# 352 tokens dense and 160 gathered in the expert layer, instead of 384 and 128, with part of the gathers among the gates

## The chip, the core and the metric

The kernel runs on one core of one Trainium2 chip. The metric is the device time of one execution in microseconds (us), read as the median of several runs. All input and output lies in the chip's memory; the span of a profile goes from the first to the last instruction.

## What is computed

Two transformer blocks on 512 tokens of width 1024, one after the other, in float32. The change touches only the last part, the expert layer. There each token chooses 128 of 16384 experts (8 heads, 16 choices each); an expert is a pair of numbers (i1, i2) from 0 to 127, with a gate g.

```
def peer_ffn(x, w_q, sub_keys, expert_u, expert_v):
    ...
    v1, i1 = lax.top_k(s1, P_TOPK)
    v2, i2 = lax.top_k(s2, P_TOPK)
    cand = (v1[..., :, None] + v2[..., None, :]).reshape(T, P_HEADS, P_TOPK * P_TOPK)
    vals, ci = lax.top_k(cand, P_TOPK)
    e = (take(i1, ci // P_TOPK) * N_KEYS + take(i2, ci % P_TOPK))
    g = jax.nn.softmax(vals, axis=-1)
    ...
        a = jnp.einsum('cd,ckd->ck', xc, expert_u[ec])
        w = (gc * jax.nn.gelu(a)).astype(x.dtype)
        return jnp.einsum('ck,ckd->cd', w, expert_v[ec])
```

The layer's output is added to the residual h.

## The kernel before

Up to about 1000 us the two blocks run (mixer, attention, projections). `peer` then works on the 512 tokens in two ways.

**Dense.** For the first NT = 384 tokens all 16384 experts are computed as 128 tiles of 128 experts. An up tile (`up_tile`) loads 512 KB of `pu`, splits it into a high and a low part (`whi` on ACT, `wlo` on DVE), runs 24 matmuls of 384 columns (lines 85 to 87, three products for each of 8 slices of the width) and applies gelu. A down step (loop over e) loads 512 KB of `pv`, splits it likewise, multiplies the tile's activations by a dense matrix of gates (`hm`, line 1544), splits the product (`xh`, `xl`, tiles `p`) and runs 18 matmuls of 512 columns into six banks `y0` to `y5`: three blocks of 128 tokens, two halves of the width, three products. 37 of the 128 up tiles are computed ahead and put away in memory (`ud`, read again as `gl`), 11 more (AHEAD) are kept on the chip (`gt`).

**The gates** (`gates`, L1443 to L1470) make the dense matrix of gates out of the choices. For each token a one-hot matrix of i1 times g and a one-hot matrix of i2 are built and multiplied on PE (L1466). One `hot` tile, a ring of six buffers named `r4`, holds four tokens: its half for i2 is built on DVE eight tokens at a time (`short`, L1457) and cast on ACT (L1460), its half for i1 by four `tensor_scalar` on DVE (L1463). ACT copies the product out of PSUM (L1467, `big`). Every 32 tokens the result (2 MB, `wd`) is written to memory; in the down loop four experts' rows of it are read again per four steps (`big<-wd`, L1537). The gates run between the last 30 of the 48 early up tiles; the other 18 lie in the loop over query projections before them.

**Gathered.** For the last 128 tokens only the chosen experts are fetched: an indirect DMA on POOL (L1493) brings one row of 4 KB for each of 128 tokens, 256 times: 128 times from `pun`, each followed by a multiply and reduce on DVE against the tokens (L1498), and 128 times from `pv`, each followed by a multiply-add on DVE into `idx` (L1508). The gathered rows use the same ring `r4` of six buffers. `work.advance` deals them out over the down loop, up to 86% over its first 80 steps, the rest over 36 more; all of them begin after the gates.

The order of instructions on each engine is fixed when the kernel is built, by a scheduler with its own table of durations; on the chip every engine takes its list in order. Weights come by SP's queue into `wraw` (3 and 2 buffers).

Of the kernel before, what the change touches and what calls it, by code (L numbers as in the profile page):

```python
# [44 lines left out]
class Builder:  # L45
# [574 lines left out]
    def attention2(self, wk, ps, h, hg):  # L620
# [480 lines left out]
        xd = self.dram.tile([128, 1024], F32, name="xd")  # L1101
# [17 lines left out]
        for b in range(4):  # L1119
# [12 lines left out]
            if b % 2 == 1:  # L1132
                for m in range(4):
# [4 lines left out]
                    for j in range(2):  # L1138
                        ts = slice(b * 128 - 128, b * 128 + 128)
                        k = 2 * m + j  # L1140
                        self.split_scaled(pt[:, j * 256:j * 256 + 256], self.gains[:, 3, k:k + 1], xn[0][k][:, ts], xn[1][k][:, ts])
        nc.gpsimd.tensor_tensor(n2b, n2b, xs[3], op=ALU.mult)
        nc.sync.dma_start(xd, n2b)
# [112 lines left out]
    def peer(self, hd, xn, xd):  # L1256
# [3 lines left out]
        NT = 384  # L1260
        AHEAD = 11
        AWAY = 37
        NREST = 4
        with ExitStack() as s5:
# [172 lines left out]
            def gates():  # L1437


                for b in range(NT // 128):  # L1440
# [3 lines left out]
                    bs = slice(b * 128, (b + 1) * 128)  # L1444
                    for n in (0, 2):
                        nc.scalar.copy(iT[n][:, bs], pt[:, n * 128:(n + 1) * 128])
                    second = wk.tile([128, 128, 8], BF16, tag="oh2", name="second", bufs=4)
                    nc.scalar.copy(second, pt[:, 128:256, None].to_broadcast([128, 128, 8]))
                    for tg in range(4):
                        wt = T("big", 2, shape=(128, 128, 32))  # L1450
                        for t4 in range(8):
                            hot = T("r4", 6, shape=(128, 2, 4, 128))
                            t0 = 128 * b + 32 * tg + 4 * t4
                            if t4 % 2 == 0:
                                short = wk.tile([128, 8, 128], BF16, tag="p", name="short", bufs=6)
                                of = second[:, t0 - 128 * b:t0 - 128 * b + 8]
                                nc.vector.tensor_tensor(short.rearrange("p t (a c) -> p t a c", c=8),  # L1457
                                                        numbers.rearrange("p (a c) -> p a c", c=8)[:, None].to_broadcast([128, 8, 16, 8]),
                                                        of[:, :, None].to_broadcast([128, 8, 16, 8]), op=ALU.is_equal)
                            nc.scalar.copy(hot[:, 1], short[:, t4 % 2 * 4:t4 % 2 * 4 + 4])  # L1460
# [15 lines left out]
            def gathered():  # L1476
                i1, i2, g = chosen(3)
# [190 lines left out]
```

## Time and profile before

| | us |
|---|---|
| median of 3 runs | 2263.39 (2263.33 to 2266.34) |
| profiled execution, its own time | 2264.04 |
| its span | 2262.3 |
| PE busy | 2207.7 (98%) |
| DVE busy | 1657.4 (73%) |
| ACT busy | 1014.1 (45%) |
| POOL busy | 724.7 (32%) |

Matmuls overlap in the records, so what one costs is read from the distance between starts, not from its duration. The DMA share is the mean busy share of the 16 DMA engines. A timeline's third column group names engine, line, operation, the tile written and the tiles read.

### The profile page before, as it was taken

The numbers are of one execution on the slowest core, as the hardware profiler recorded it, in microseconds if no ns is written. First come the engines' busy times: TensorE is split into PE (matmuls) and PEld (weight loads), VectorE is DVE, ScalarE is ACT, GpSimd is POOL, SyncE is SP. The second block draws the span as 40 slices with busy tenths as digits, with TensorE's granted clock in tenths as the row PEclk, the third lists the DMA queues.
The fourth block names the chain that finished last, engine by engine and source line by source line (L and its number), as shares of the span: only waits on it lengthen the run. The fifth ranks groups of instructions, "written<-read, shape, count | busy, mean of one in ns | idle before, by whom it ended". The sixth has DMA issues, their size and how long they took to land.

```text
span 2262.3 us, 32117 instructions
## 1 busy us (share of the span) xinstructions
PE 2207.7 (98%) x11327; PEld 1927.8 (85%) x11327; DVE 1657.4 (73%) x3611; ACT 1014.1 (45%) x1781; POOL 724.7 (32%) x731
## 2 busy tenths in 40 slices
PE   7999999999999889989999999999999999999999
PEld 5888888888878757879999998999999999998887
DVE  7875666543357688769889986888888888888654
ACT  4544444432244578853237764333333333333332
POOL 1221111000013756735640002544445444444000
PEclk9999999999999999989999999999999999999999
DMA  4222222243333212154445667999999999999874
GB/s 131 80 80 84 84 77 82 88 136 94 94 96 119 87 49 80 65 178 130 133 137 176 250 214 295 352 339 349 338 337 345 333 336 347 344 334 351 271 230 126
DMA packets 171443, 439.57 MB, mean 194 GB/s; under 512 B 15121, under 2 KB 74001, under 8 KB 169745
## 3 DMA queue, kind: packets, MB, share of 16 engines
q1 hardware_dynamic: 129088, 296.00, 40.3%
q0 software_dynamic: 36864, 134.23, 16.1%
q10 hardware_dynamic: 5328, 7.28, 0.9%
q8 instruction: 89, 1.46, 0.3%
q14 instruction: 74, 0.60, 0.1%
HBM read 395.05 MB, written 41.35 MB: 193 GB/s over the span
## 4 chain that ended last, share of the span: by engine, by line
PE 88%; DVE 6%; ACT 2%; issue 2%; DMA 1%; POOL 1%; SPq 0%; DVEq 0%; POOLq 0%; ACTq 0%
PE mm L87 13%; PE mm L86 13%; PE mm L85 13%; PE y L85 8%; PE y L86 8%; PE y L87 8%; PE y L1466 4%; PE g L87 3%; PE g L86 3%; PE g L85 3%; PE s L377 2%; PE pt L403 2%; PE o L407 1%; PE o L406 1%; PE wo L86 1%
## 5 line engine op out<-in xcount | busy, mean ns | idle before, releaser
L66 ACT CAST whi<-wraw 128x1024 fp32r<-128x1024 f32 (+2 forms) x413 | 430.4, 1043 | 977.3 <-PE mm L86 395.3
L72 DVE TENSOR_TENSOR wlo<-wraw,whi 128x1024 fp32r<-128x1024 f32 x368 | 456.8, 1241 | 255.6 <-ACT whi L66 255.3
L87 PE MATMUL mm<-uh,wlo 128*128 128x384 f32 (+1 forms) x1616 | 578.1, 358 | 3.7 <-DVE wlo L72 3.7
L85 PE MATMUL mm<-uh,whi 128*128 128x384 f32 (+1 forms) x1616 | 580.0, 359 | 0.3 <-DVE ul L154 0.3
L86 PE MATMUL mm<-ul,whi 128*128 128x384 f32 (+1 forms) x1616 | 578.7, 358 | 0.0
L85 PEld LDWEIGHTS mm<-uh,whi 128*128 128x128 f32 x1616 | 304.5, 188 | 26.3 <-DVE ul L154 0.7
L87 PEld LDWEIGHTS mm<-uh,wlo 128*128 128x128 f32 x1616 | 304.5, 188 | 25.7 <-DVE wlo L72 4.0
L86 PEld LDWEIGHTS mm<-ul,whi 128*128 128x128 f32 x1616 | 304.6, 188 | 25.2
L85 PE MATMUL y<-whi,p 128*128 128x512 f32 x768 | 300.7, 392 | 0.2 <-ACT p L66 0.2
L86 PE MATMUL y<-wlo,p 128*128 128x512 f32 x768 | 300.4, 392 | 0.0
L87 PE MATMUL y<-whi,p 128*128 128x512 f32 x768 | 291.4, 390 | 0.0
L1493 POOL DMA_INDIRECT r<-pun_in,row x128 | 167.1, 1305 | 362.7 <-DVE act L1498 175.0
L1493 POOL DMA_INDIRECT r<-pv_in,row x128 | 171.1, 1337 | 185.3 <-DVE idx L1508 163.4
L72 POOL TENSOR_TENSOR wlo<-wraw,whi 128x1024 fp32r<-128x1024 f32 (+3 forms) x45 | 100.9, 2247 | 304.9 <-ACT whi L66 304.8
L87 PEld LDWEIGHTS y<-whi,p 128*128 128x128 f32 x768 | 144.2, 188 | 32.1
L85 PEld LDWEIGHTS y<-whi,p 128*128 128x128 f32 x768 | 144.2, 188 | 29.0 <-ACT p L66 0.6
L86 PEld LDWEIGHTS y<-wlo,p 128*128 128x128 f32 x768 | 144.3, 188 | 27.4
L1498 DVE CUSTOM_DVE_ANT_0 r<-r,val 128x1024 f32<-128x1024 f32 x128 | 153.9, 1220 | 13.5 <-DMA r<-pun_in,row 13.5
L1508 DVE SCALAR_TENSOR_TENSOR idx<-r,act,idx 128x1024 f32<-128x1024 f32 x127 | 162.9, 1283 | 1.1
L72 DVE TENSOR_TENSOR p<-p 128x384 fp32r<-128x384 f32 x128 | 71.3, 557 | 93.5 <-PE y L86 90.5
L382 ACT ACTIVATE p<-p,st 128x128 f32<-128x128 f32 (+3 forms) x160 | 89.7, 562 | 72.6 <-DVE st L381 71.0
L1463 DVE TENSOR_SCALAR r<-iota,iT,iT 128x128 f32<-128x128 f32 x384 | 102.6, 360 | 15.7 <-PE y L1466 15.7
(603 smaller groups left out, 3584.9 us busy)
## 6 DMA issues: line engine op xcount, KB each, us to landing
wraw<-w_in SPq DMA_DIRECT2D x145, 512.0 KB, 3.6
wraw<-pu_in SPq DMA_DIRECT2D x128, 512.0 KB, 5.4
wraw<-pv_in SPq DMA_DIRECT2D x128, 512.0 KB, 5.5
wd<-big SPq DMA_DIRECT2D x12, 2048.0 KB, 7.2
big<-wd SPq DMA_DIRECT2D x31, 768.0 KB, 7.3
ud<-gs ACTq DMA_DIRECT2D x37, 192.0 KB, 2.2
gl<-ud SPq DMA_DIRECT2D x37, 192.0 KB, 2.8
hd<-h SPq DMA_DIRECT2D x24, 256.0 KB, 2.3
```

What stands on the lines that cost most here:

```text
L66: nc.scalar.copy(hi, src)
L72: i = eng.tensor_tensor(lo, src, hi, op=ALU.subtract)
L85: mm(out, w[0], x[0], start=start, stop=False)
L86: mm(out, w[0], x[1], start=False, stop=False)
L87: mm(out, w[1], x[0], start=False, stop=stop)
L377: nc.tensor.matmul(s[:, :n], q[:, b], k[:, :n], start=t == 0, stop=t == len(qk) - 1)
L382: nc.scalar.activation(pi, pi, AF.Exp, bias=st[:, 0:1], scale=-1.0, accum_out=st[:, 1:2])
L1463: nc.vector.tensor_scalar(hot[:, 0, t], iota, i1, g, op0=ALU.is_equal, op1=ALU.mult)
L1466: nc.tensor.matmul(wp[:, t * 128:(t + 1) * 128], hot[:, 0, t], hot[:, 1, t], start=True, stop=True)
L1493: nc.gpsimd.indirect_dma_start(t, None, src, bass.IndirectOffsetOnAxis(ap=rows[n][:, s:s + 1], axis=0))
L1498: nc.vector.tensor_tensor_reduce(t, t, xn3, 1.0, 0.0, ALU.mult, ALU.add, act[:, s:s + 1])
L1508: nc.vector.scalar_tensor_tensor(yg[0], t, act[:, s:s + 1], yg[0], op0=ALU.mult, op1=ALU.add)
```

## The change

`NT` becomes 352, and the last 32 of the third block's tokens join the gathered ones. Up tiles run matmuls of 352 columns, the third token block of a down step has 96 tokens, and the gates have 88 hot tiles instead of 96 and 11 matrices to write instead of 12.

The 32 tokens are laid out as four quarters on 128 rows (`quarters`: row 32q + t holds token t's choices 32q to 32q + 31), so that 32 gathers from `pun` and 32 from `pv` do them; twelve small DMAs of 32x32 and four of 32x1024 set this up. A matmul with `fold` adds the four quarters, and the sum is added to `h` and written out. Then follow the 128 tokens as before. There are 320 gathers in all; `picked.advance` deals 15% of them (48) out over the 30 up tiles among the gates, then up to 85% over the 80 first down steps, and the rest over 45 more.

In the gates the half of a hot tile for i1 is built by ACT from a second `short` (a copy with scale g) for tokens 0 to 7 of every 16, and by DVE as before for the others.

```diff
-        nc.sync.dma_start(xd, n2b)
+        nc.sync.dma_start(xd[:128], n2b)
+        nc.sync.dma_start(xd[128:], xs[2][96:128])
...
-        NT = 384
+        NT = 352
+        INGATES = 0.15
...
                             if t4 % 2 == 0:
...
+                                s2 = short(1, t0 - 128 * b)
+                                s1 = short(0, t0 - 128 * b) if t4 % 4 == 0 else None
+                            half = t4 % 2 * 4
+                            nc.scalar.copy(hot[:, 1], s2[:, half:half + 4])
                             for t in range(4):
                                 i1, g = (iT[n][:, t0 + t:t0 + t + 1] for n in (0, 2))
-                                nc.vector.tensor_scalar(hot[:, 0, t], iota, i1, g, op0=ALU.is_equal, op1=ALU.mult)
+                                if s1 is None:
+                                    nc.vector.tensor_scalar(hot[:, 0, t], iota, i1, g, op0=ALU.is_equal, op1=ALU.mult)
+                                else:
+                                    nc.scalar.activation(hot[:, 0, t], s1[:, half + t], AF.Copy, scale=g)
...
+            def quarters(tag, src, dt=F32):
+
+                t = T(tag, 1, dt, (128, 32))
+                for q in range(4):
+                    nc.sync.dma_start(t[32 * q:32 * q + 32], src[96:128, 32 * q:32 * q + 32])
+                return t
...
+            def gathered():
+                rows = [quarters(f"rq{n}", r, I32) for n, r in enumerate(rows_of(2))]
+                g = quarters("gq", chosen(2)[2])
...
+                yield from gather(rows, xg, T("actq", shape=(128, 32)), g, part)
...
+                    nc.tensor.matmul(p, fold, part[:, cs], start=True, stop=True)
+                    nc.vector.tensor_tensor(h[96:128, cs], h[96:128, cs], p[96:128], op=ALU.add)
+                nc.sync.dma_start(self.out[352:384], h[96:128])
+                rows = rows_of(3)
+                xg = T("val", shape=(128, 1024))
+                nc.sync.dma_start(xg, xd[:128])
+                yg[0] = T("idx", shape=(128, 1024))
+                yield from gather(rows, xg, T("act", shape=(128, 128)), chosen(3)[2], yg[0])
...
+            picked = Work(gathered(), 320)
             for n, e in enumerate(rest_tiles):
                 work.advance((n + 1) / len(rest_tiles))
                 up_tile(e, "dve")
+                picked.advance((n + 1) / len(rest_tiles) * INGATES)
...
-                work.advance((e + 1) / steps * 0.86 if e < steps else 0.86 + (e + 1 - steps) / 36 * 0.15)
+                picked.advance(INGATES + (0.85 - INGATES) * (e + 1) / steps if e < steps else 0.85 + (e + 1 - steps) / 45 * 0.16)
```

What the scheduler makes of it is seen at three places. The first is PE at the end of the gates. `y` with `r` is a hot tile, `mm` an up tile, `y` with `whi,p` the first down step. Before:

```order
L87 MATMUL mm<-uh,wlo_13639 128x384
L1466 MATMUL y_13676<-r_13670 128x128 x4
L1466 MATMUL y_13690<-r_13682 128x128 x4
L1466 MATMUL y_13702<-r_13696 128x128 x4
L85 MATMUL mm<-uh,whi 128x384
...
L86 MATMUL mm<-ul,whi_13782 128x384
L85 MATMUL y_13741<-whi,p 128x512
```

And with the change, at the same place:

```order
L85 MATMUL mm<-uh,whi_13907 128x352
L1480 MATMUL y_13271<-r_13263 128x128 x4
L86 MATMUL mm<-ul,whi_13907 128x352
L87 MATMUL mm<-uh,wlo_13908 128x352
L1480 MATMUL y_13283<-r_13277 128x128 x4
L1480 MATMUL y_13335<-r_13325 128x128 x4
...
L1480 MATMUL y_13821<-r_13815 128x128 x4
L85 MATMUL y_13866<-whi,p 128x512
```

Before, the hot tiles come three at a time between up tiles, and a whole up tile stands between the last of them and the first down step. With the change the up tiles end earlier: 21 hot tiles (y_13283 to y_13821) stand behind the last matmul of an up tile, with nothing between them, and the first down step follows at once.

The second place is DVE in the middle of the gates, with the change. `actq` is the multiply and reduce of a gathered row; before, these stand in the down loop and the gates hold only the other kinds.

```order
L1475 TENSOR_SCALAR r_11976<-iota,iT_11436,iT_11438 128x128 x4
L1457 TENSOR_TENSOR short<-numbers,eights 128x1024 x2
L1521 ISA r_11956,actq<-r_11956,val 128x1024
L1521 ISA actq 128x1
L1521 ISA r_11959,actq<-r_11959,val 128x1024
L1457 TENSOR_TENSOR short<-numbers,eights 128x1024
L72 TENSOR_TENSOR wlo_12802<-wraw,whi_12801 128x1024
```

In the whole stretch from the first `short` to the first down step's multiply, DVE has 176 `tensor_scalar` (380 before), 66 `short` (48), 24 `wlo` (22), 32 reduces and 14 multiply-adds of gathered rows (1 and 0).

The third place is DVE late in the down loop, at steps 95 and 96, before:

```order
L1544 TENSOR_TENSOR p<-gl,big 128x384
L72 TENSOR_TENSOR wlo<-wraw,whi 128x1024
L72 TENSOR_TENSOR p<-p 128x384
L1567 TENSOR_TENSOR r_21170<-r_21170,idx 128x512 x2
L1544 TENSOR_TENSOR p<-gl,big 128x384
```

And with the change, at steps 100 and 101:

```order
L1531 SCALAR_TENSOR_TENSOR idx<-r_20532,act,idx 128x1024
L1593 TENSOR_TENSOR p<-gl,big 128x352
L1531 SCALAR_TENSOR_TENSOR idx<-r_20567,act,idx 128x1024
L72 TENSOR_TENSOR wlo<-wraw,whi 128x1024
L72 TENSOR_TENSOR p<-p 128x352
L1531 SCALAR_TENSOR_TENSOR idx<-r_20602,act,idx 128x1024
L1531 SCALAR_TENSOR_TENSOR idx<-r_20637,act,idx 128x1024
```

Before, the last gathered row is consumed ahead of step 94's multiply, and 23 of the 256 stand behind step 80's. With the change the last one stands ahead of step 114's, and 54 of the 320 stand behind step 80's: 19 up to step 91's, 35 from there on.

## Rows read from the trace of the kernel before

**Rows 1.** Busy time by stage: us, then busy (count) per engine, PE clock, DMA share, GB/s

```profile
1000.00:1180.00 180.00, 179.94 (x991) 164.95 (x989) 153.44 (x809) 59.88 (x85) 98.04 (x103) 1.00 0.43 130
1214.00:1300.00 86.00, 86.00 (x655) 85.97 (x653) 86.00 (x264) 69.80 (x132) 0.00 (x0) 1.00 0.62 229
1500.00:1600.00 100.00, 100.00 (x509) 91.15 (x509) 82.45 (x121) 35.35 (x49) 47.91 (x37) 1.00 0.96 340
```

**Rows 2.** Who waited for whom, 1180 us to the end: total us, times, longest

```profile
DVE r L1498 <- DMA r<-pun_in,row: 13.5, 3, 7.9
...
PE mm L87 <- DVE wlo L72: 3.7, 1, 3.7
```

**Rows 3.** Timeline of PE: start us, duration us, engine, line, operation

```profile
1599.98 0.34 PE L87 MATMUL mm<-uh,wlo 128*128 128x384 f32 x1
...
1603.79 0.39 PE L85 MATMUL y<-whi,p 128*128 128x512 f32 x1
...
1607.91 0.33 PE L85 MATMUL mm<-uh,whi 128*128 128x384 f32 x1
...
1306.86 2.84 PE L1466 MATMUL y<-r 128*128 128x128 f32 x24
1309.45 0.42 PE L85 MATMUL mm<-uh,whi 128*128 128x384 f32 x1
...
765.46 0.28 PE L87 MATMUL f<-whi,cx 128*64 128x256 f32 x1
...
766.49 0.28 PE L87 MATMUL f<-whi,cx 128*64 128x256 f32 x1
```

**Rows 4.** Timeline of DVE among the gates

```profile
1233.17 6.25 DVE L1463 TENSOR_SCALAR r<-iota,iT,iT 128x128 f32<-128x128 f32 x24
1239.32 1.90 DVE L1457 TENSOR_TENSOR short<-numbers,second 128x1024 bf16<-128x1024 bf16 x3
1241.12 2.37 DVE L72 TENSOR_TENSOR wlo<-wraw,whi 128x1024 fp32r<-128x1024 f32 x2
```

**Rows 5.** Timeline of DVE and of its groups: a gathered row's reduce, and its multiply-add

```profile
1602.10 1.22 DVE L1498 CUSTOM_DVE_ANT_0 r<-r,val 128x1024 f32<-128x1024 f32 x1
...
L1508 DVE SCALAR_TENSOR_TENSOR idx<-r,act,idx 128x1024 f32<-128x1024 f32 x127 | 162.9, 1283 | 1.1
```

**Rows 6.** Timeline of ACT: among the gates, and scaled copies before them

```profile
1225.21 1.08 ACT L66 CAST whi<-wraw 128x1024 fp32r<-128x1024 f32 x1
1226.16 0.52 ACT L1382 ACTIVATE gs<-mm 128x384 f32<-128x384 f32 x1
...
1232.06 0.61 ACT L1467 COPY big<-y 128x512 f32<-128x512 f32 x1
1232.53 0.65 ACT L1460 CAST r<-short 128x512 f32<-128x512 bf16 x1
1233.05 0.61 ACT L1467 COPY big<-y 128x512 f32<-128x512 f32 x1
...
988.22 0.47 ACT L153 ACTIVATE uh<-s,gains 128x256 fp32r<-128x256 f32 x1
988.59 0.71 ACT L1131 ACTIVATE p<-h,r 128x512 f32<-128x512 f32 x1
```

**Rows 7.** DMA queues and gathers, 1500 to 2040 us: packets, MB, share; issues, us to landing

```profile
q0 software_dynamic: 27891, 101.55, 51.2%
q1 hardware_dynamic: 45172, 81.81, 44.2%
...
r<-pv_in,row POOLq DMA_INDIRECT x110, 6.6
r<-pun_in,row POOLq DMA_INDIRECT x85, 6.9
```

**Rows 8.** DMA queue of SP, 2140 to 2200 us: packets, MB, share of 16 engines

```profile
q1 hardware_dynamic: 9568, 13.10, 73.7%
```

**Rows 9.** Busy time of a stretch as in Rows 1, with the densest transfers

```profile
1400.00:1460.00 60.00, 56.32 (x276) 50.92 (x275) 47.32 (x71) 20.32 (x28) 26.99 (x19) 0.97 1.02 374
```

More of the change, by code (lines that the diff above doesn't have):

```diff
@@ L1437, in gates @@
             def gates():
-                for b in range(NT // 128):
+                for b in range(3):
                     pt = P("y2")
@@ L1443, in gates, with short @@
                         nc.tensor.transpose(pt[:, n * 128:(n + 1) * 128], t, self.ident)
-                    bs = slice(b * 128, (b + 1) * 128)
+                    nb = min(128, NT - b * 128)
                     for n in (0, 2):
[L1446 to L1449, printed above, removed]
+                        nc.scalar.copy(iT[n][:, b * 128:b * 128 + nb], pt[:, n * 128:n * 128 + nb])
+                    eights = [wk.tile([128, 128, 8], BF16, tag="oh2", name="eights", bufs=4) for _ in range(2)]
+                    for n in range(2):
+                        nc.scalar.copy(eights[n], pt[:, n * 128:n * 128 + 128, None].to_broadcast([128, 128, 8]))
+                    def short(n, t):
+                        x = wk.tile([128, 8, 128], BF16, tag="p", name="short", bufs=6)
+                        nc.vector.tensor_tensor(x.rearrange("p t (a c) -> p t a c", c=8),
+                                                numbers.rearrange("p (a c) -> p a c", c=8)[:, None].to_broadcast([128, 8, 16, 8]),
+                                                eights[n][:, t:t + 8, None].to_broadcast([128, 8, 16, 8]), op=ALU.is_equal)
+                        return x
+                    for tg in range(nb // 32):
                         wt = T("big", 2, shape=(128, 128, 32))
@@ L1474, in peer, with rows_of @@
             yg = [None]
[L1476 to L1477 removed]
+            def rows_of(b):
+                i1, i2, _ = chosen(b)
                 rows = []
[L1479 removed]
+                for n, (x, z) in enumerate(((i1, i2), (i2, i1))):
                     t = T("rf", 1, shape=(128, 128))
[L1481 removed]
+                    nc.vector.scalar_tensor_tensor(t, x, 128.0, z, op0=ALU.mult, op1=ALU.add)
                     ri = T(f"row{n}", 1, I32, (128, 128))
@@ L1521, in advance @@
                             self.done += c
-            work = Work(gates(), 3 * 32 * 0.8)
+            work = Work(gates(), NT // 4 * 0.8)
+            picked = Work(gathered(), 320)
             rest_tiles = list(first_tiles)
@@ L1531, in peer @@
             y = [[P(f"y{2 * b + c}") for c in range(2)] for b in range(3)]
-            work = Work(gathered(), 256 * 1.2)
             for e in range(128):
```

59 lines of the change are left out of this document (32 added, 27 removed).

## Prediction

> **What bounds the kernel now.** I read the busy times by stage first, then who waited for whom, then distances between starts. From 1000 us on PE is busy throughout: 179.94 of 180 us in the loop over queries, 86 of 86 among the gates, 100 of 100 in the down loop [rows 1]. Behind 1180 us it waited for DVE once, 3.7 us [rows 2], at the start of the down loop, where DVE itself waited for gathered rows, 13.5 us in three waits [rows 2]. So the expert layer's time is PE's own sum, and what shortens PE's list shortens the kernel, as long as no other engine comes out longer. Two are near: DVE, with 86 of 86 us in the first half of the gates and 82 of 100 later, and the DMA engines, with a share of 0.96 in the down loop against 0.62 among the gates [rows 1]. The change takes work from PE and gives work to ACT, DVE and DMA in just these stages.
>
> **What a matmul costs.** From 1599.98 to 1603.79 us lie 22 matmuls of 384 columns, 0.1732 us each, from there to 1607.91 us 18 of 512, 0.2289 each [rows 3]. No row has 352 columns. The line through 384 and 512 gives 0.1593, that through 256 (nine in 1.03 us, 0.1144 each [rows 3]) and 384 gives 0.1585. I take 0.159: 0.0142 less than now, 0.34 us for an up tile of 24. A record of a hot tile's matmul costs 0.108 (24 in 2.59 us [rows 3]), and a hot tile has eight of them, 0.86 us. The 18 matmuls of a down step keep their 512 columns: that one block has 96 tokens instead of 128 shortens only its weight load, so nothing is gained there.
>
> **Early up tiles.** 18 lie in the loop over queries, where PE is full and DVE has 27 us of 180 free [rows 1]: 18 x 0.34 = **-6.1**.
>
> **The gates.** Before, PE has 24 up tiles of 4.16 us and 96 hot tiles beside them: 99.8 + 82.9 = 182.7 us. DVE, counted from the order: 380 `tensor_scalar` at 0.256, 48 `short` at 0.60, 22 `wlo` at 1.19 [rows 4] and one gathered row make 153 us. ACT: 96 x 0.99 for the cast and the copy of a hot tile, some 23 `whi` at 0.95, as many gelus at 0.52 [rows 6] and three copies of 1024 elements make 132 us. PE is the longest by 30 us.
>
> With the change PE has 24 x 24 x 0.159 + 704 x 0.108 = 167.6 us. DVE: 176 x 0.256 + 66 x 0.60 + 24 x 1.19 + 32 reduces at 1.22 + 14 multiply-adds at 1.28 [rows 4, 5] = 170 us. ACT: 88 x 0.99 + 24 x 0.95 + 23 x 0.52 + 6 x 0.95, and 176 scaled copies of 128 elements. The trace has none of these; the nearest is one of 256 elements, 0.37 us to the next start [rows 6], which is the upper bound. Less 128 elements at the slope between 512 elements (0.52) and 1024 (0.95) [rows 6] it is 0.26, which I take. ACT then has 173 us, at the upper bound 193. So three engines stand within 6 us of each other, and the order shows what follows: 21 hot tiles are left on PE without any up tile beside them. There a tile takes ACT 0.99 + 2 x 0.26 = 1.51 us against PE's 0.86, so PE idles 21 x 0.65 = 14 us; some 2 us more go by while ACT copies the last tile out, DVE multiplies and ACT casts for the first down step. 167.6 + 14 + 2 = 183, where it was 182.7: what PE saves here is given back, **0**. The lower bound is the longest engine without any waiting, 173 (-9); the upper bound adds 20 for the dearer scaled copy (65 instead of 46 us) or for waits of like size.
>
> The 48 gathers here share the ring of six buffers with the hot tiles. From release to landing a gather takes about 7 us [rows 7], and by the order DVE has mostly 10 to 16 us of other work between the use of the buffer's last tenant and that of the gathered row. This is the cover for the landing, so I price the waits at nothing; if it is gone, DVE waits, and behind it `wlo` and the next hot tiles, so PE too. The `val` load from `xd` stands on SP's queue ahead of weight loads and waits for the last of the 32 reduces; the up tiles behind it have five `wraw` buffers, so this I put at 0 as well.
>
> **The down loop.** 80 up tiles: 80 x 0.34 = **-27.2**. Per step PE has 7.93 us instead of 8.28, and DVE, busy for 82 of 100 us before [rows 1], consumes 2.85 gathers in it instead of 2.99. For DMA one gather takes 0.512 x 540 / 195 = 1.42 us of all engines, a step's loads by SP 0.442 x 540 / 65.2 = 3.66 us [rows 7]. With the change: 3.59 + 2.85 x 1.42 = 7.6 of 7.93 us, a share of 0.96 as before. Nothing is lost there. The fold costs PE two matmuls of 512 columns in full precision; at the hot tile's 0.216 for 128 columns that is 4 x 0.216 x 2 = **+1.7**, and its store on SP's queue waits for DVE, behind which five weight buffers cover. The stumble at the start of the loop, 3.7 us of waiting [rows 2] and a clock of 0.97 over 60 us [rows 9], I leave as it is.
>
> **The end of the down loop.** From step 80 on there are no up tiles, and a step is 18 x 0.2289 = 4.12 us. DMA per step: between 2140 and 2200 us, without gathers, SP's queue has a share of 0.737 [rows 8], 3.04 us of a step; with 352 tokens 2.92, and 2.17 before the `gl` loads set in (1.42 for the weights and 11/12 of the 0.82 that remain of a step's 3.66 without two weight loads). By the order 54 gathers are consumed in steps 80 to 113, of which six are under way at its start. 11 x 2.17 + 23 x 2.92 + 48 x 1.42 = 159 us of DMA against 34 x 4.12 = 140 us of PE: 19 us too much. Before, the same sum for steps 80 to 93 gives 10 x 2.24 + 4 x 3.04 + 17 x 1.42 = 58.7 against 57.7 us, and PE did not wait. Of the 19 us the five weight buffers take up some 6 (four loads at 1.42), and DVE's lead of one to two steps over PE 6 more; **+7** remains, between 0 and 19. DVE, with 1.5 multiply-adds at 1.28 and a `wlo` at 1.19, has 3.1 of 4.12 us there before its two tiles of 352 columns, so it can hardly catch up.
>
> Over the 60 us from 1400 us the DMA engines moved 374 GB/s at a share of 1.02 [rows 9]; the last 34 steps' bytes (34 x 0.70 + 23 x 0.18 + 48 x 0.524 = 53 MB) would take 142 us at that rate, 2 over PE's. The Trainium skill, page "DMA: Bandwidth & Descriptors", section "Specifications", gives about 358 GB/s as the limit of HBM for a core. The trace passes it here, on one core alone; by the page's figure the stretch would take 149 us, 9 too many before any cover, and the term would be 0 instead of 7.
>
> **The sum.** -6.1 + 0 - 27.2 + 1.7 + 7 = -24.6, against the profiled execution's 2264.04 us (its span of 2262.3 and 1.7 around it): 2239.4. It lies 0.65 above the median of the runs, 2263.39, so the time is **2239 us**.
>
> **Rivals.**
>
> *All of it is kept.* ACT, DVE and PE overlap among the gates and the DMA excess is covered: -6.1 - 9 - 27.2 + 1.7 + 0 = -41, 2223; with PE alone deciding the gates (-15) 2217. For it: PE never waited there before [rows 1]. Against: the 21 hot tiles at the end of PE's list.
>
> *Most of it is given back.* Gates at +20 and the end at +12: -6.1 + 20 - 27.2 + 1.7 + 12 = 0, about 2263, no change. For it: a scaled copy at 0.37; a share of DMA that hardly went past 1.02 [rows 9].
>
> *Slower: the gathers among the gates land late.* In the ring of six, a gathered row that comes late holds DVE, whose list holds the next hot tiles and `wlo`. At the start of the down loop three waits made 13.5 us [rows 2]; were each of the 48 gathers here to cost 1 us beyond the sum above, the time would be 2239 + 48 = 2287. It decides from 0.6 us per gather on (29 us, past 2268). The 2 MB writes of `wd` lie between the gathers and could cause it; the 10 to 16 us of cover speak against it.
>
> *It doesn't do what it says: 352 columns start no sooner than 384.* The weight load would set the distance. Then 33 us of the gain are gone: 2272. Against: 256, 384 and 512 columns lie on one line [rows 3].
>
> **How the numbers follow.** The forecast (2226 to 2253) has 0.62, all kept 0.18, most given back 0.10, late gathers 0.07, no shorter matmul 0.03. The range leaves out half of the first rival's lower end, the late gathers and the last, and goes over the bounds of gates and end: **2218 to 2263**. A measurement here tells about 0.2%, 4.5 us, from no change: faster than 2259 is the forecast, the first rival and three in ten of the second (0.83); within 2259 to 2268 the rest of it and a little of the late gathers (0.08); slower 0.09.
>
> **What the profile after would show.** Starts 0.159 us apart in up tiles; the down loop's 80 common steps 7.93 us each. Among the gates ACT and DVE near full, and PE with gaps in front of the first down step, its hot tiles there 1.5 us apart. Behind step 91 a DMA share of 1.0 and DVE waiting for `pv` rows. The prediction is wrong if DVE waits for `pun` rows among the gates, if scaled copies start 0.37 us apart or more, or if PE loses more than 19 us behind step 80.

## Result and profile after

The changed kernel takes 2279.26 us (median of 7 runs, 2274.03 to 2288.31), the kernel before beside it 2266.73 us: a ratio of 1.0058, 95% interval 1.0047 to 1.0068. It is slower by 0.6%; the forecast was 2239 us, between 2218 and 2263. The profiled execution took 2279.26 us, its span is 2277.5 (2262.3 before).

Five marks on PE's timeline divide the expert layer: the first projection of its query loop (994.51 us, before 993.31), the first transposition of the gates (1201.17, 1201.71), the first matmul of the down loop (1414.96, 1392.04), the last matmul of an up tile at step 79, and the last matmul of the down loop.

| stage, us | before | after | change | forecast |
|---|---|---|---|---|
| query loop with early up tiles | 208.4 | 206.7 | -1.7 | -6.1 |
| gates, to the first down matmul | 190.3 | 213.8 | +23.5 | 0 |
| down loop with up tiles | 667.0 | 640.2 | -26.8 | -25.5 |
| down loop behind them | 198.1 | 217.8 | +19.7 | +7 |

So the loop gained about what was forecast, and the gain was lost on both sides of it. Busy time by stage, after, with the columns of [rows 1] (the engines are PE, its weight loads, DVE, ACT and POOL):

```profile
1000.00:1180.00 180.00, 178.72 (x1007) 163.33 (x1006) 157.49 (x827) 60.54 (x86) 99.89 (x136) 0.99 0.44 137
1200.00:1340.00 140.00, 137.95 (x994) 136.89 (x993) 119.75 (x250) 127.30 (x289) 41.09 (x32) 1.00 0.88 311
1340.00:1400.00 60.00, 49.10 (x332) 45.94 (x330) 51.99 (x109) 53.73 (x129) 23.09 (x18) 0.94 0.89 328
1400.00:1420.00 20.00, 5.04 (x13) 3.80 (x14) 10.10 (x14) 1.97 (x5) 9.18 (x8) 0.57 0.97 372
1500.00:1600.00 100.00, 100.00 (x528) 88.61 (x527) 82.39 (x122) 36.38 (x51) 38.74 (x35) 1.00 0.97 345
...
2110.00:2190.00 80.00, 68.91 (x286) 51.46 (x285) 66.64 (x76) 23.33 (x32) 30.42 (x24) 0.98 0.99 351
```

And before, at the end of the gates and behind step 80:

```profile
1340.00:1400.00 60.00, 59.77 (x401) 58.65 (x400) 36.39 (x96) 33.43 (x58) 11.17 (x10) 1.00 0.70 244
2110.00:2190.00 80.00, 80.00 (x351) 65.47 (x350) 45.26 (x61) 28.62 (x39) 0.00 (x0) 1.00 0.77 235
```

PE is full in the middle of the loop as before, but not at the end of the gates (49 of 60 us, then 5 of 20) nor behind step 80 (69 of 80). Who waited, from 1180 us on for PE and up to 1415 us for DVE, against [rows 2]:

```profile
PE y L85 <- ACT p L66: 29.6, 9, 15.4
PE y L1480 <- DVE r L1475: 5.1, 4, 3.0
PE y L1480 <- ACT r L1471: 4.1, 5, 1.3
PE y L1480 <- ACT r L1477: 3.0, 5, 0.8
...
DVE r L1521 <- DMA r<-pun_in,rq: 19.0, 12, 4.4
DVE idx L1531 <- DMA r<-pv_in,rq: 10.9, 5, 5.8
```

PE's waits for the cast of the split product (`p`) are one of 15.4 us at the first down step, and eight behind step 80, 14.2 us together. The first, as PE, SP, DVE and ACT show it:

```profile
1397.47 2.05 PE L1480 MATMUL y<-r 128*128 128x128 f32 x16 [0.98 <-ACT r L1471]
1414.96 0.79 PE L85 MATMUL y<-whi,p 128*128 128x512 f32 x1 [15.44 <-ACT p L66]
...
1398.72 0.38 SPq L1586 DMA_DIRECT2D big<-wd  x1
...
1404.31 1.28 DVE L1531 SCALAR_TENSOR_TENSOR idx<-r,actq,idx 128x1024 f32<-128x1024 f32 x1 [0.74 <-DMA r<-pv_in,rq]
1411.40 1.28 DVE L1531 SCALAR_TENSOR_TENSOR idx<-r,actq,idx 128x1024 f32<-128x1024 f32 x1 [5.81 <-DMA r<-pv_in,rq]
1413.90 0.49 DVE L1593 TENSOR_TENSOR p<-gt,big 128x320 f32<-128x320 f32 x1 [1.22 <-DMA big<-wd]
...
1414.43 0.48 ACT L66 CAST p<-p 128x352 fp32r<-128x352 f32 x1 [14.28 <-DVE p L1593]
```

Two things come late together. On DVE's list a gathered row stands ahead of the first step's multiply (L1593), and it lands at 1411.4. The gates that the multiply reads (`big<-wd`) are asked for only at 1398.72, when the last matrix but one has been written to memory, and land 1.2 us after the row is done with. Both also land slowly. Issues from 1398.8 to 1407 us, KB each, median us to landing:

```profile
wd<-big SPq DMA_DIRECT2D x1, 2048.0 KB, 18.8
big<-wd SPq DMA_DIRECT2D x1, 640.0 KB, 15.2
r<-pv_in,rq POOLq DMA_INDIRECT x6, 13.3
```

The gathers there take twice the 6.6 us of the down loop [rows 7], beside the write of the gates' last matrix and the read of the others.

Behind step 80, ACT, PE and DVE around one of the eight waits:

```profile
2126.43 1.04 ACT L66 CAST whi<-wraw 128x1024 fp32r<-128x1024 f32 x1 [3.20 <-PE y L87]
2127.38 0.48 ACT L66 CAST p<-p 128x352 fp32r<-128x352 f32 x1
...
2127.91 0.50 PE L85 MATMUL y<-whi,p 128*128 128x512 f32 x1 [1.56 <-ACT p L66]
...
2124.40 1.28 DVE L1531 SCALAR_TENSOR_TENSOR idx<-r,act,idx 128x1024 f32<-128x1024 f32 x1
2125.60 0.52 DVE L1593 TENSOR_TENSOR p<-gl,big 128x352 f32<-128x352 f32 x1
2127.50 1.23 DVE L72 TENSOR_TENSOR wlo<-wraw,whi 128x1024 fp32r<-128x1024 f32 x1 [1.39 <-ACT whi L66]
```

ACT waits until PE's last matmul of a step frees the buffer for a later step's weight cast (`whi`), and the cast that PE needs for its very next step stands behind it on ACT's list: PE waits for both, 1.04 + 0.48 us. Seven of the eight waits are of this kind, 1.52 to 1.56 us each.

### The profile page after: what moved, and what is told of

It is laid out like the page before. It is cut to its first block, busy times and chain, and to the rows that moved or that the text cites. A ratio compares the mean times of both kernels' runs of the same rounds, so it can differ in the third digit from the quotient of the medians.

```text
span 2277.5 us, 32231 instructions
## 1 busy us (share of the span) xinstructions
PE 2182.3 (96%) x11267; PEld 1868.0 (82%) x11267; DVE 1682.2 (74%) x3526; ACT 1048.9 (46%) x1945; POOL 777.1 (34%) x796
## 5 line engine op out<-in xcount | busy, mean ns | idle before, releaser
L85 PE MATMUL mm<-uh,whi 128*128 128x352 f32 (+1 forms) x1616 | 567.3, 351 | 1.2 <-ACT gs L1385 0.9
L86 PE MATMUL mm<-ul,whi 128*128 128x352 f32 (+1 forms) x1616 | 566.8, 351 | 0.0
L87 PE MATMUL mm<-uh,wlo 128*128 128x352 f32 (+1 forms) x1616 | 565.0, 350 | 0.1
L85 PE MATMUL y<-whi,p 128*128 128x512 f32 (+1 forms) x768 | 305.0, 399 | 29.6 <-ACT p L66 29.6
L86 PE MATMUL y<-wlo,p 128*128 128x512 f32 (+1 forms) x768 | 303.4, 395 | 0.0
L87 PE MATMUL y<-whi,p 128*128 128x512 f32 (+1 forms) x768 | 283.2, 394 | 0.0
L1521 DVE CUSTOM_DVE_ANT_0 r<-r,val 128x1024 f32<-128x1024 f32 x160 | 193.9, 1219 | 19.1 <-DMA r<-pun_in,rq 19.0
L85 PEld LDWEIGHTS y<-whi,p 128*128 128x128 f32 (+1 forms) x768 | 138.8, 181 | 67.1 <-ACT p L66 33.5
L87 PEld LDWEIGHTS y<-whi,p 128*128 128x128 f32 (+1 forms) x768 | 137.5, 179 | 40.3
L86 PEld LDWEIGHTS y<-wlo,p 128*128 128x128 f32 (+1 forms) x768 | 138.9, 181 | 37.3 <-issue 0.4
L72 DVE TENSOR_TENSOR p<-p 128x352 fp32r<-128x352 f32 x128 | 67.1, 524 | 77.6 <-PE y L86 72.8
L1480 PE MATMUL y<-r 128*128 128x128 f32 x704 | 97.7, 285 | 12.5 <-DVE r L1475 5.1
```

The lines of the kernel that those rows point to most:

```text
L72: i = eng.tensor_tensor(lo, src, hi, op=ALU.subtract)
L85: mm(out, w[0], x[0], start=start, stop=False)
L86: mm(out, w[0], x[1], start=False, stop=False)
L87: mm(out, w[1], x[0], start=False, stop=stop)
L1480: nc.tensor.matmul(wp[:, t * 128:(t + 1) * 128], hot[:, 0, t], hot[:, 1, t], start=True, stop=True)
L1521: nc.vector.tensor_tensor_reduce(t, t, xg, 1.0, 0.0, ALU.mult, ALU.add, act[:, s:s + 1])
```

## Experiments

All times are medians beside runs of the kernel before on the same chip; the ratio is to these. "Gates" here is from the first to the last hot tile, "gap" PE's time from there to the first down matmul, "tail" from the last up tile's last matmul to the last down matmul. These four are read from one profiled execution each, whose own time can lie off the median beside it: for e8 2266.7 us, for e15 2249.8, for e17 2261.6.

| kernel | gates | gap | loop | tail | median, us | ratio [95%] |
|---|---|---|---|---|---|---|
| before | 173.1 | 5.3 | 667.0 | 198.1 | | 1 |
| after | 184.2 | 15.4 | 640.2 | 217.8 | 2279.3 | 1.0058 [1.0047, 1.0068] |
| e1_dense | 161.0 | 5.5 | 644.0 | 209.9 | 2241.3 | 0.9888 [0.9872, 0.9905] |
| e2_onchip | 183.5 | 13.5 | 639.8 | 217.7 | 2276.8 | 1.0036 [1.0019, 1.0052] |
| e3_nogates | 169.0 | 22.3 | 646.0 | 232.7 | 2301.7 | 1.0158 [1.0141, 1.0175] |
| e4_notail | 184.5 | 16.0 | 640.1 | 199.9 | 2264.6 | 0.9990 [0.9977, 1.0003] |
| e5_order | 186.9 | 14.0 | 639.6 | 213.7 | 2274.2 | 1.0028 [1.0013, 1.0043] |
| e6_hold | 180.8 | 13.2 | 640.2 | 220.5 | 2280.2 | 1.0059 [1.0043, 1.0076] |
| e7_holdchip | 183.9 | 2.4 | 642.0 | 225.2 | 2275.0 | 1.0034 [1.0021, 1.0046] |
| e8_best | 184.8 | 2.6 | 640.0 | 216.3 | 2261.5 | 0.9980 [0.9970, 0.9990] |
| e9_thindve | 187.2 | 14.2 | 639.8 | 209.1 | 2271.4 | 1.0027 [1.0016, 1.0039] |
| e10_thindma | 182.2 | 15.5 | 639.8 | 199.9 | 2261.7 | 0.9984 [0.9966, 1.0002] |
| e11_dvegates | 203.0 | 7.2 | 641.8 | 222.9 | 2297.3 | 1.0138 [1.0121, 1.0155] |
| e12_best3 | 207.8 | 3.0 | 647.3 | 212.3 | 2285.2 | 1.0079 [1.0059, 1.0098] |
| e13_gatesthin | 178.1 | 4.1 | 641.1 | 217.7 | 2261.3 | 0.9979 [0.9967, 0.9990] |
| e14_paced | 189.1 | 2.1 | 638.2 | 213.8 | 2266.9 | 0.9996 [0.9986, 1.0006] |
| e15_spread | 177.9 | 3.1 | 641.5 | 201.8 | 2255.0 | 0.9954 [0.9938, 0.9971] |
| e16_tailonly | 183.2 | 16.8 | 640.2 | 200.1 | 2262.9 | 0.9984 [0.9974, 0.9993] |
| e17_all | 187.8 | 3.1 | 640.8 | 202.0 | 2253.0 | 0.9940 [0.9923, 0.9956] |

The kernel before had medians of 2265.2 to 2267.0 us beside these runs. In before and e1 the gap is not idle but matmuls of an up tile. Gates of the same code differ by up to 10 us between executions: e8, e15 and e17 have it alike, and DVE waits there 20.5, 13.2 and 23.9 us for `pun` rows. The changed kernel's own gates, in the six executions that share them (after, e4, e5, e9, e10, e16), have 182.2 to 187.2 us.

**e1_dense: the dense part alone.**

```diff
-                                s1 = short(0, t0 - 128 * b) if t4 % 4 == 0 else None
+                                s1 = None
...
-                picked.advance((n + 1) / len(rest_tiles) * INGATES)
```

> The dense part of the change alone: NT = 352, the gates built by DVE as before, the 128 tokens gathered as before (all behind the gates). The 32 other tokens' gathers are left out; rows 352 to 383 of the output hold only the residual. If the prediction's dense terms are right (early tiles -6, the gates' PE sum 168 instead of 183 us, 80 up tiles -27), the time is 2264 - 48 = 2216, at most 2225. If the dense part itself loses what the change lost (a worse order of the gates, lower clock), it is 2240 or more.

A miss of the theory: 2241.3. The other number, 2240 or more, fits, but not its reason: the gates took 12 us less than before (15 forecast) and the loop 23 less. What was lost lies in the tail, 11.8 us more, though nothing was added to it. In the order, 38 gathered rows are consumed behind step 80 here, 23 before, with the same rule of dealing them out. That shorter steps let fewer rows through in the loop is the likely reason; no run tests it.

**e2_onchip, e6_hold, e7_holdchip: what held the first down step.** The first copies the four experts' rows of the last written matrix on the chip, so that they need no round trip through memory:

```diff
+                        w8 = T("w8", shape=(128, 2, 4, 32))
+                        load = nc.sync.dma_start(w, wd[:8, :, 0:4, :].rearrange("g p e t -> p g e t"))
+                        nc.sync.dma_start(w8[:, 0], wd[8, :, 0:4, :])
+                        nc.scalar.copy(w8[:, 1], last[1][:, 0:4])
```

> The changed kernel, but the first four down steps no longer wait for the gates' last matrix but one to be written to memory and read again: its four rows are copied on the chip by ACT, and the other nine matrices, written long before, are read into a tile of the ring r4 and a small one. All gathers keep their places. Theory A (the round trip through memory holds the first down step): the gap of PE before it falls from 15.4 us to about 3, and with the half-clock stretch behind it the time falls by 12 to 15, to 2264 to 2267. Theory B (the gathered rows ahead of the first multiply on DVE's list hold it, the last of which landed at 1411.4): the gap falls to 11 to 13 us and the time by 2 to 4, to about 2276.

Theory B: the gap is 13.5 us and the median fell by 2.4 (ratio 1.0036 against 1.0058; their intervals overlap). The row now lands at 1412.2, and the multiply follows at once (DVE's timeline):

```profile
1412.21 1.28 DVE L1531 SCALAR_TENSOR_TENSOR idx<-r,actq,idx 128x1024 f32<-128x1024 f32 x1 [4.62 <-DMA r<-pv_in,rq]
1413.41 0.42 DVE L1600 TENSOR_TENSOR p<-gt,r 128x256 f32<-128x256 f32 x1
```

The second takes the rows away instead, and keeps the round trip:

```diff
-        INGATES = 0.15
+        INGATES = 0.11
...
-                picked.advance((n + 1) / len(rest_tiles) * INGATES)
+                picked.advance(min((n + 1) / 22, 1) * INGATES)
...
+                    with self.in_order(begun):   # begun: the first down step's multiply
+                        nc.vector.tensor_tensor_reduce(...)
```

> The changed kernel with 35 instead of 48 gathers among the gates, all dealt out over the first 22 of the 30 up tiles, and DVE's work on later rows kept behind the first down step's multiply; 13 more gathers in the down loop. The round trip of the gates through memory stays. DVE has 17 us less among the gates. If the gathered rows ahead of the first multiply were all (theory B of the run with the copy on the chip), the gap before the first down step falls from 15.4 to about 3 us and with 5 us from DVE's shorter list the time is about 2261. If the round trip holds it just as long (both are late together), the gap is still 9 to 13 us and the time 2268 to 2274.

The gap stays, 13.2 us, and DVE now waits for the gates alone. The time did not fall (2280.2, where 2268 to 2274 had been expected); 9 more rows came to lie behind step 80 (63 for 54), and the tail is 2.7 us longer. Waits from 1385 to 1410 us:

```profile
DVE p L1596 <- DMA big<-wd: 11.2, 1, 11.2
```

> Both edits together: no gathered row ahead of the first multiply on DVE, and the first four steps' gates without the round trip through memory. If these two, each late by itself, made the gap, it falls to about 3 us, no half-clock stretch follows, and the time is 2258 to 2264 (12 from the gap, 2 from the clock, 5 from DVE's shorter list, less 3 for the 13 gathers that end up behind step 80). If the gap stays over 8 us, a third thing holds the first step.

With both edits the gap is 2.4 us:

```profile
1403.64 0.64 PE L85 MATMUL y<-whi,p 128*128 128x512 f32 x1 [2.37 <-ACT p L66]
```

So either cause alone holds the step for 13 us, and only both together free it. The time forecast for this kernel was a miss (2275.0): 67 rows now lie behind step 80, and the tail has 225.2 us.

**e3_nogates: no gather among the gates.**

```diff
-        INGATES = 0.15
+        INGATES = 0.0
```

> The changed kernel with no gather among the gates (INGATES = 0, so 272 instead of 224 gathers in the first 80 down steps). Theory A (the 48 gathers cost little among the gates, the end of the gates and the round trip cost most): from the first transposition of the gates to the first down matmul it takes 213.8 us in the changed kernel; without gathers DVE has 53 us less there, so at most 15 us go, to about 199. The rival of the prediction (late gathers, about 0.5 to 1 us each): 24 to 48 us go, to 166 to 190. Behind it the loop must take longer in both: 3.4 gathers a step at 1.42 us of DMA and 3.59 us of SP's loads make 8.4 us a step instead of 7.95, 38 us over 80 steps: total about 2300 by theory A, 2270 to 2290 by the rival.

The total is that of theory A (2301.7), by luck. The gates fall by 15.2 us, 0.32 per gather. But the gap grows to 22.3 us: seven rows of the loop came to stand ahead of the first multiply on DVE's list, and DVE waited 15.5 us for them there. And the loop, for which 38 us more had been reckoned from DMA, took 5.8 us more: only 227 rows are consumed in it, 92 behind step 80, where the tail is 14.9 us longer, and 12 us more go by behind the last matmul.

**e4_notail: the last 48 gathers left out.**

```diff
-(... if e < steps else 0.85 + (e + 1 - steps) / 45 * 0.16)
+(... if e < steps else 0.85)
```

> The changed kernel with the last 48 gathers left out (nothing is fetched for them from step 80 on, so the sum of the 128 gathered tokens lacks these choices). Theory A (the gathers behind step 80 hold DVE and so ACT's cast of the split product): the waits of PE for ACT's cast there go, 14 us, and the time is 2263 to 2266. Rival (they come from the order of ACT's weight cast and its split cast alone, or from the loads by SP): PE still waits 7 us or more there and the time is 2271 or more.

Theory A: no waits, tail 199.9, 2264.6 us. The tail is 1.8 us longer than before (47 steps of 4.167 instead of 4.128), so the rows behind step 80 cost 17.9.

**e5_order: the order of ACT's casts behind step 80.**

```diff
+                with self.in_order([halves[e - 2]] if e >= 80 else []):   # ACT's split cast of step e - 2
                     c = self.chunk(self.i["pv"][e])
```

> The changed kernel with one order imposed from step 80 on: on ACT's list the weight cast of step e stands behind the split cast of step e - 2. Every gather, load and multiply stays. In the changed kernel PE waits there in eight places for the split cast, seven of them 1.52 to 1.56 us, which is a weight cast (1.05) and a split cast (0.48) one behind the other, where ACT had waited for PE's last matmul of the step before to release the weight cast's buffer. Theory A (the order of ACT's two casts makes the waits): they go, 14 us and the low clock behind them, and the time is 2262 to 2266. Theory B (DVE or the DMA engines come late, the order only shows it): PE waits as long at the same steps and the time is 2274 or more.

By the time theory B, by the waits between the two: they fell from 14.2 to 8.3 us, the tail by 4.1, the time to 2274.2. ACT now waits for DVE's multiply instead (ACT's timeline):

```profile
2150.49 0.48 ACT L66 CAST p<-p 128x352 fp32r<-128x352 f32 x1 [4.97 <-DVE p L1596]
```

**e8_best: e7 with that order.** 

> The same with the order of ACT's casts from step 80 on as well. If the two explanations (gap ahead of the down loop, order of the casts behind step 80) are right and add up: 14 to 20 us less than without that order, 2242 to 2248, below the kernel before. If the order is not the cause: as without it, about 2261.

The order gave 13.5 us on the same chip (2275.0 to 2261.5), near the forecast of 14 to 20, of which the tail has 8.9. The sum missed: 2261.5 instead of 2242 to 2248, since e7 had already missed by 14. (That 2261 is also the number given for "not the cause" is chance; it was reckoned from e7's forecast.)

**e9_thindve and e10_thindma: DVE's work or the transfers behind step 80.** Both with the order of e5.

```diff
+                        c = slice(0, 32 if late[0] else 1024)   # e9; late: dealt out from step 80 on
...
+                    t = fetch(pv, 1, s, 16 if late[0] else 128)   # e10: rows fetched
```

> The changed kernel with the order of ACT's casts as in the run before it that imposed this order, and with DVE's multiply-adds of the rows dealt out from step 80 on made on 32 of 1024 columns (the other columns of these choices are left out of the sum). The gathers themselves, and all other transfers, stay. With the full multiply-adds it took 213.7 us from the last matmul of an up tile to the last of the down loop, without these gathers 199.9. Theory A (DVE's list is too long behind step 80): 200 to 203, time about 2262. Theory B (the DMA engines are the limit there, share 1.0): 210 or more, time 2270 or more.

> The reverse: the gathers dealt out from step 80 on fetch 16 rows instead of 128 (an eighth of the bytes); DVE's multiply-adds keep their full size, on another tile, with a small one on the fetched rows. What the 112 other tokens would have had from these choices is wrong. Theory A (DVE): 211 or more from the last up matmul to the end of the down loop. Theory B (DMA): 200 to 203, time about 2262.

By their numbers theory B in e10 (199.9); in e9 theory B by the time (2271.4), neither by the tail (209.1). From 2110 to 2190 us, e9 and then e10:

```profile
2110.00:2190.00 80.00, 74.97 (x308) 56.37 (x307) 42.25 (x79) 25.33 (x34) 22.29 (x24) 0.96 1.03 368
...
2110.00:2190.00 80.00, 80.00 (x347) 61.96 (x346) 75.45 (x110) 28.95 (x39) 52.15 (x25) 1.00 0.86 242
```

DVE with 75 of 80 us held nobody in e10. But with thin transfers the builder's scheduler had also spread the rows differently, 1.3 a step up to step 117 instead of 1.8 up to step 109. The pair does not tell transfers from density. What held PE in e9 its trace shows: three waits of 5.0 us together, the two longer ones behind a row that landed 1.5 us late and behind a load of `gl` (DVE's timeline), and 6.8 us at half clock:

```profile
2173.85 0.52 DVE L1598 TENSOR_TENSOR p<-gl,big 128x352 f32<-128x352 f32 x1 [3.73 <-DMA gl<-ud]
```

So with the rows at 1.8 a step, transfers do come late there once DVE is fast.

**e15_spread, e16_tailonly, e17_all: the same rows, spread out.** In e15 and e17 on top of e8, in e16 on the changed kernel with the order of e5 alone (there with 0.83 and 0.173 for 0.8 and 0.203):

```diff
-(0.85 - INGATES) * (e + 1) / steps if e < steps else 0.85 + (e + 1 - steps) / 45 * 0.16)
+(0.8 - INGATES) * (e + 1) / steps if e < steps else 0.8 + (e + 1 - steps) / 45 * 0.203)
...
+                if e >= 80:
+                    begun[:] = [first]   # rows dealt out in step e stand behind its multiply
```

> The kernel with the three edits, and behind step 80 the same 67 gathered rows spread out: 1.45 rows a step up to step 124 (before 1.76 a step up to step 117), each row's multiply-add behind the multiply of the step that deals it out. Nothing is left out. DVE then has 2.2 + 1.45 x 1.28 = 4.1 of 4.17 us a step. Theory A (behind step 80 DVE's list is too long): from the last up matmul to the end of the down loop it falls from 216.3 to 200 to 205 us, and the time to about 2248. Theory B (the transfers are too many): 61 x 1.42 us of gathers and 129 us of SP's loads make 216 us of DMA for 196 us of PE however they are spread, so it stays at 211 to 219 and the time at 2256 to 2264.

> The changed kernel up to step 80 as it is, gap and all; behind step 80 the order of ACT's casts, and the same 54 rows spread out at 1.2 a step up to step 124, each behind the multiply of the step that deals it out. Nothing is left out. If the density of the rows on DVE's list and the order of the casts are the whole of the loss behind step 80, the 217.8 us from the last up matmul to the end fall to 200 to 203 and the time by 15 to 18, to 2261 to 2264. If the loss needs the other edits too (it came from the gap's late start), 210 or more and 2270 or more.

> The kernel with all edits again, beside the one before it on the same chip: the difference between the two is what the gap at the start of the down loop and 13 gathers fewer among the gates are worth, 12 us of gap, 2 of the half clock and up to 5 of the gates. Expected 2250 to 2257, against 2261 to 2264 for the one before it.

Theory A by the tail, in all three: 201.8, 200.1 and 202.0 us with every row and byte in place. (e15's time, 2255.0, is 7 above the number given with it.) In e16 DVE's list up to step 80 is that of the changed kernel, and PE has no wait behind it; from 2110 to 2190 us, e16 and then e15:

```profile
2110.00:2190.00 80.00, 80.00 (x347) 61.96 (x346) 65.39 (x79) 28.62 (x38) 30.14 (x22) 1.00 0.99 352
...
2110.00:2190.00 80.00, 78.91 (x340) 60.25 (x339) 70.61 (x83) 28.87 (x38) 35.05 (x27) 1.00 1.04 381
```

e16's DMA share is that of the changed kernel, 0.99, and PE is full. Its time, 2262.9, is 16.4 below the changed kernel's median (15 to 18 forecast). e17 beside it on the same chip is 9.9 lower, within what was expected, though its terms add up to 19; at 0.9940 [0.9923, 0.9956] it is faster than the kernel before. Three things changed together behind step 80: the order of ACT's casts, how densely the rows stand, and that each stands behind a step's multiply. The first alone brought 4.1 us of the tail (e5); the other two were not separated.

**e11_dvegates: the i1 halves back on DVE.** `s1 = None`, as in e1.

> The changed kernel with all of the gates' halves for i1 built by DVE as before (no scaled copies on ACT); the 48 gathers stay among the gates. DVE has 176 x 0.256 - 22 x 0.60 = 32 us more there, ACT 58 less. If DVE with the waits for gathered rows sets the gates' length, the gates (184.2 us from the first to the last hot tile) take 205 to 216 and the time is 2300 to 2311. If ACT sets it, they take 175 to 190 and the time is 2270 to 2285.

The gates are 18.8 us longer, the time 18: DVE decides, though both lie a little below the range given for it.

```profile
PE y L1480 <- DVE r L1475: 23.9, 18, 4.5
```

**e13_gatesthin: rows among the gates that hardly move bytes.**

```diff
+                    n = 16 if thin[0] else 128
...
+                        nc.gpsimd.indirect_dma_start(t[:n], None, src, ...)
```

> The changed kernel, but the 48 gathers among the gates fetch 16 rows instead of 128 (an eighth of the bytes), while DVE's multiplies over all 128 rows keep their size, on another tile, with a small one on the fetched rows (what the 32 tokens get is wrong). Between the first and the last hot tile it took 184.2 us with the 48 gathers and 169.0 without any. If the waits for late landings make the 15 us (the rival of the prediction, with 0.3 us each instead of 1), 169 to 174 remain; if DVE's 57 us of work on the rows does, 180 to 185.

Neither bound: gates 178.1. Of the 15.2 us that the 48 gathers cost there, 6.1 go with their bytes (4 to 9 against the spread of the changed kernel's gates above); DVE waits 14.6 us for rows instead of 29.9, and the gap falls from 15.4 to 4.1. Gates and gap together are 17.4 us shorter, 0.36 per gather, and the time 18. (The order of the rows differs a little: 46 instead of 48 ahead of the first multiply.)

**e12_best3 and e14_paced: two misses.** e12 puts 48 rows among the first 24 up tiles on top of e8, e14 puts ACT's casts of a hot tile behind the copying-out four tiles before.

> The changed kernel with the three edits (first gates from the chip, no gathered row ahead of the first multiply, order of ACT's casts), but with all 48 gathers among the gates, dealt out over the first 24 of the 30 up tiles instead of 35 over 22. Against that run 13 gathers move from behind step 80 to the gates: if each costs 0.25 to 0.33 us behind step 80 and 0.32 among the gates, the time is the same, 2259 to 2264; if DVE's waits for the rows among the gates cost more, 2265 to 2270.

> The kernel with the three edits (gates of the first steps from the chip, no gathered row ahead of the first multiply, order of ACT's casts behind step 80) and one more order on ACT: the casts and scaled copies of a hot tile stand behind the copying-out of the product four hot tiles before. In the kernel with three edits PE waits 4.0 and 3.5 us for these copies late in the gates, where ACT has four hot tiles' casts ahead of them. Theory (ACT's list makes these two waits): they go, the gates fall from 184.8 to about 178 us, and the time is 2252 to 2258, faster than both kernels. Rival (ACT is too long there in any order): the waits only move, and the time stays at 2259 to 2264.

e12: the gates grow to 207.8 us. More rows in less time make DVE wait 31 us for them there (24.6 in e8), and PE 27 us in all for hot tiles; a time of 2259 to 2270 had been expected. e14: PE's two waits for the copying-out (7.5 us in e8) become four, 5.0 us together, but the sum of the gates' waits is 16.7 for 13.5; the rival, that the waits only move, fits, but the time, 2266.9, is above its range too.

## Why the prediction was wrong

**The price of a matmul: right. The loop: near, in part by luck.** 24 matmuls of 352 columns take 3.84 us, 0.160 each (0.159 forecast), and this step 7.99 us:

```profile
1599.08 0.39 PE L85 MATMUL y<-whi,p 128*128 128x512 f32 x1
...
1603.23 0.32 PE L85 MATMUL mm<-uh,whi 128*128 128x352 f32 x1
...
1607.07 0.39 PE L85 MATMUL y<-whi,p 128*128 128x512 f32 x1
```

Its 18 matmuls take 4.15 us for 4.12 [rows 3]; a third block of 96 tokens makes them no faster. On average a step takes 8.00 us, where it was 8.28 and I had 7.93: 79 steps give -22, not -27. The stumble at the start [rows 2], which I had left in, did not come back and made up for most of it (in e1, whose loop began as early as before, it did, 3.6 us). The DMA share of 0.97 is near the 0.96 forecast.

**The early tiles: -1.7 for -6.1.** 574 up matmuls stand ahead of the mark instead of 563, 1.8 us that moved. Waits of 1.2 and 0.9 us and a stretch at half clock (0.91 over 20 us, at most 1.8 us) more than cover the rest.

**The gates: the term 0 became +23.5.** Of these, 11.1 us lie between the first and the last hot tile, 10.1 from there to the first down matmul, 2.2 ahead of both. PE's sum held: PE's own work shrank by 13.5 us (602 matmuls at 0.160 and 76 us of hot tiles, for 594 at 0.173 and 83), and the 21 hot tiles at the end took 33.2 us, 1.58 each, where I had 1.51. The scaled copy takes 0.30 us to the next start (four in 1.18 us), between my 0.26 and its bound 0.37. The Trainium skill, page "ScalarE: Activation LUTs", section "What ACT_TABLE_LOAD costs", gives 186 ns and 0.833 for each element, 93 more for an operand from a tile and an overlap of 93 back to back: an estimate of 0.29 for 128 elements. The trace agrees.

Two steps failed. First, "some 2 us more go by while ACT copies the last tile out, DVE multiplies and ACT casts": it was 15.4, and 2 more in the loop for its first ten matmuls, which came 0.43 us apart, at half the clock. I had counted DVE's list up to a small multiply of 32 columns (L1595); three more rows, the late one among them, stand behind it and ahead of the one that PE needs (L1593). I followed the computation across the seam and not the lists: what stands ahead of the first multiply on DVE, and when the gates that it reads can have been written. The order in the section on the change shows that no up tile is left to bridge it.

Second, "I price the waits at nothing" for the gathers here. DVE waited 29.9 us for them, and the 48 cost 15.2 us of gates (e3) and, with the gap, 17.4 us by their bytes alone (e13). The cover of 10 to 16 us was counted on DVE's list, the landing of 7 us taken from the down loop. But here the 30 `pun` gathers issued from 1215 us on took 8.0 us to land (median), the six at the seam 13.3, and rows came up to 5.8 us late. Some were asked for late as well, since POOL had to wait until hot tiles had been read and their buffers of the ring were free:

```profile
1393.69 1.86 POOL L1516 DMA_INDIRECT r<-pv_in,rq  x1 [3.90 <-PE y L1480]
```

The sum that I made for the loop I did not make here: a share of 0.62 [rows 1] and 48 x 1.42 us over 214 make 0.94; it is 0.88 to 0.97. Such a share alone costs nothing, as e16 shows behind step 80, but a landing time read elsewhere does not hold in it. My third rival's reason, the 2 MB writes between the gathers, fits the 13.3 us at the seam, where one was under way; no run leaves the writes out.

**The end: +19.7 for +7, and for another reason.** I reckoned that transfers exceed PE's time by 19 us and that buffers cover 12. The size of 17.9 lies in my bounds, by luck; the mechanism does not hold. Behind step 80 DVE waits for no `pv` row at all, though I had said it would; its waits are for ACT's weight cast (25.8 us) and for PE. Of PE's eight waits seven come from ACT's order, and in the eighth (3.4 us) ACT waits for DVE's multiply. e16 moves the same bytes with no wait of PE, and e15's rows, at my 1.42 us each, need 216 us of DMA together with SP's loads, in a tail of 201.8. I had read a share of 1.0 as the end of what can be had; it went to 1.04 at 381 GB/s. The Trainium skill, page "DMA: Bandwidth & Descriptors", section "Specifications", gives about 358 GB/s as the limit of HBM for a core; over these 80 us the trace passes it by 6%. (The 149 us that the prediction works out from it are 148.)

What cost the time was how the rows stand on DVE's list, 1.8 a step, two or three at a time ahead of a multiply, and ACT's casts in the wrong order behind that. I had also misread the order: the last row stands ahead of step 110's multiply, not of step 114's, so the 54 rows lie in 30 steps and not 34. With that the DMA sum would have been 24 us too much instead of 19, and my sum for DVE is 1.8 x 1.28 + 1.19 + 2 x 0.52 = 4.5 us in a step of 4.12: DVE alone is over PE, where I wrote 3.1 before two tiles and drew from it only that DVE can hardly catch up. (In e15, at 1.5 rows a step, the same sum gives 4.2, and nearly nothing is lost.) DVE is not the whole of it at that density: thin work took 4.6 us of 13.8 away (e9), and 9.2 stayed, there with late transfers.

**The rivals.** "Most of it is given back" came nearest: gates at +20 and the end at +12 were +23.5 and +19.7. Its reasons, a scaled copy at 0.37 us and a DMA share that cannot rise, were not the causes. "Late gathers" named one of the true causes and its side of the result, at 0.36 us per gather instead of 1; by itself it stays under the 0.6 from which it was to decide. The order in which the instructions stand was no term of the sum, and it made most of the error: e17, which changes only order, dealing and one round trip through memory, takes 26 of the 40 us back.

## What to carry over

- At a seam between two stages, take the first instruction of the next stage on each engine, and list what stands ahead of it there, gathered rows and round trips through memory among it. Where two things are late together, taking one away shows nothing.
- Sum a helping engine's list step by step over the steps in which its extra work really stands, and look where it stands. The 54 rows were dear in 30 steps, two or three in a row ahead of what the busiest engine waits for; over 44 steps, each behind a step's multiply and with ACT's casts in order, they were free.
- Look for a cast that waits for the busy engine to free a buffer, ahead of one that this engine waits for: each such pair cost about both casts here, 1.5 us.

## Unexpected of the hardware

The DMA engines moved 381 GB/s over 80 us at a share of 1.04 beside a PE that was busy for 78.9 of them (e15). A gather of 128 rows landed after 6.6 us (median) in the down loop before the change and after 13.3 us at the seam, beside the write and the read of the gates. After 15.4 us without work PE's first ten matmuls came 0.43 us apart instead of 0.23, at 1.2 instead of 2.4 GHz; the granted clock from 1415 to 1419 us is 0.50:

```profile
1415.00:1419.00 4.00, 4.00 (x10) 3.02 (x11) 4.00 (x8) 1.25 (x3) 1.48 (x1) 0.50 0.92 373
```
